# The last down-projection of an encoder trunk: the eleventh channel pair moved into the seven-product scheme, and the final norm moved into the plan

## The chip, the cores and the metric

The kernel runs on one core of a Trainium2 chip. The metric is the device time of one execution in microseconds (us), as the median of several runs. The engines named here are PE (TensorE, the matrix array), DVE (VectorE), ACT (ScalarE), POOL (GpSimd) and SP (SyncE, whose queue issues nearly all DMAs). SBUF is the on-chip memory, PSUM the small memory into which PE writes.

## The reference

A trunk of two layers over 1024 tokens of width 1024, all in float32. Each layer has a token mixer (attention in layer 0, pooling in layer 1), a cross-attention into 256 memory tokens and a gated feed-forward block; a final norm ends it. What matters here is the feed-forward block and the end:

```python
def conv_gated_ffn(h, w_up, conv_w, conv_b, w_down):
    u = h @ w_up                                   # 1024 -> 2 x 2816
    up = jnp.pad(u, ((0, 0), (1, 1), (0, 0)))
    u = up[:, :-2] * conv_w[0] + up[:, 1:-1] * conv_w[1] + up[:, 2:] * conv_w[2] + conv_b
    gate, val = u[..., :D_FF], u[..., D_FF:]
    return (jax.nn.silu(gate) * val) @ w_down      # 2816 -> 1024
...
        x = x + conv_gated_ffn(rmsnorm(x, ffn_norm[i]), ffn_w_up[i], ffn_conv_w[i],
                               ffn_conv_b[i], ffn_w_down[i])
    return rmsnorm(x, final_norm)
```

## The kernel before

**Numbers.** Each float32 operand is split into a high part (ACT, `high`) and a low part (DVE, `low`); a product of two operands is three matmuls (`mm3`: high by high, high by low, low by high). The residual stream is eight row tiles X0 to X7 of 128 tokens x 1024 columns in SBUF.

**Seven products.** The large projections are done by a scheme of Strassen's kind: a 2 x 2 product of blocks takes seven block products instead of eight, for some extra sums of operands. `PRODUCTS` names for each product its left and right operand, the PSUM bank it is added to (x, y or z), and the output that is read from that bank when it is done: "g" is the even row tile of a pair, "v" the odd one, 0 or 1 the column half. Products 2, 1 and 5 start a bank; 6, 3, 7 and 4 add to one. Each read (`read`, an add on DVE) adds the bank as it stands to the output.

**The feed-forward block** (`ffn_main`). The up-projection runs over 22 blocks f of 128 channels; behind it the convolution (ACT and DVE), the gate, and for each pair q = (2q, 2q+1) of blocks the left operands of the down-projection: four sums on DVE and seven stores of 256 KB into G7 in DRAM (`plan_gated`, `plan_sums`, `keep`). The even block of such a pair is kept in X4, the sums in X6, two row tiles that are not needed then (their rows lie in Xd in DRAM). The right operands, sums of quarters of `ffn_w_down`, were made earlier, during the cross-attention, and stored in WT (`down_sums`; `SUMS_AT` says at which weight blocks of that stage).

**Rounds.** The down-projection goes over ten pairs in three rounds (`ROUNDS`: 3, 4 and 3 pairs). In a round, for each group g of four row tiles, each of the seven products is done for two pairs of row tiles (j = 0, 1), over all pairs of the round; `plan_G` fetches and splits left operands, `plan_W` right ones, `plan_down` emits 3 matmuls of 512 columns for each pair and one read. Operands lie in 40 half tiles of SBUF: a pair's seven right operands take seven, a left operand takes two.

**The eleventh pair** (blocks 20 and 21) is done as a plain product: the gated blocks go to G (two stores of 512 KB), come back with two blocks of `ffn_w_down` (`plan_operand`), and `gemm` and `add` do 6 matmuls and one add for each row tile and column half. In layer 0 this work is handed to the next stage. In layer 1 `run` does it at the end, row tile by row tile, with the final norm one row tile behind: square on ACT (`row_rstd`), two small POOL operations, the multiply by row factor and gain on DVE (`last`, in two halves for row tile 7), and the store.

**The order of work** is not left to the engines. `Plan` takes operations with a cost per kind, gives each a due time (PE work in the order entered; others the latest time that PE's work allows, or a `late` given with them; none at all if nothing on PE follows), and emits each engine's instructions in the order in which its model would start them: the earliest possible start first, unless something with an earlier due time would be held up. Each engine, and SP's queue of DMAs, then runs its own list in order.

Of the kernel before, what the change touches and what calls it, by code (L numbers as in the profile page):

```python
# [16 lines left out]
P = 128  # L17
# [30 lines left out]
NQ = NF // 2 - 1  # L48
ROUNDS = ((0, 1, 2), (3, 4, 5, 6), (7, 8, 9))
# [579 lines left out]
class Kernel:  # L629
# [530 lines left out]
    def cross(self, i, X, steps=None, mixer=None, over={}):  # L1160
# [211 lines left out]
        def main():  # L1372
# [70 lines left out]
    def down_sums(self, i):  # L1443
# [3 lines left out]
        WT = self.WT[i] = [self.tc.dram_tile([4, P, 512], F32, name=f"Wt{i}_{q}") for q in range(NQ)]  # L1447
        raws, todo = {}, iter(range(NQ))

# [69 lines left out]
    def ffn(self, i, lhs, X, free, rhs, free_w, extra=None):  # L1519
# [6 lines left out]
        return self.ffn_main(i, U, X, Xd, extra, partial(U.begin, *self.rows_by(lhs, X, free, rhs, free_w), self.conv_table(i)))  # L1526

    def ffn_main(self, i, U, X, Xd, extra, begin):
        nc, R = self.nc, self.R
        wd = self.a["ffn_w_down"][i]  # L1530
        G = self.tc.dram_tile([2 * P, S], F32, name=f"G{i}")
        G7 = self.tc.dram_tile([NQ, P, 7 * 512], F32, name=f"Gs{i}")
# [25 lines left out]
        def held(name, f):  # L1558

            return name == "v" and f % 2 == 0 and f < 2 * NQ  # L1560
# [21 lines left out]
        def plan_gated(plan, f, late):  # L1582
            g, v = conv("g", f), conv("v", f)
            plan.add("add", 1024, partial(gated, f), g + v, v, uses=g + v, late=late)
            if f >= 2 * NQ:
                q = f - 2 * NQ
# [36 lines left out]
        def plan_G(plan, r, qs, g, n):  # L1623

            raw, parts, w = ("graw", r, g, n), [("g", r, g, n, j) for j in range(2)], len(qs) * 256
            at = PLACE.index(n) * 512 + g * 256

            def fetch():
                GA[raw] = self.scr()
                nc.sync.dma_start(out=GA[raw][:, :w].rearrange("p (q c) -> p q c", c=256),  # L1630
                                  in_=G7[qs[0]:qs[-1] + 1, :, at:at + 256].rearrange("q p c -> p q c"))

            def high():
                hs = GA[r, g, n] = [R.get_half(), R.get_half()]
                self.high(R.hv(hs[0])[:, :w], GA[raw][:, :w])

            def low():
                h, l = (R.hv(h)[:, :w] for h in GA[r, g, n])
                self.low(h, l, GA.pop(raw)[:, :w])
            plan.add("load", len(qs) / 4, fetch, [("G", q, n) for q in qs], [raw], [("scr", raw)])  # L1640
            plan.add("copy", w, high, [raw], parts, [("half", k) for k in parts], [raw])
            plan.add("add", w, low, [raw, *parts], parts, uses=[raw, *parts])
            plan.ended[parts[1]] = lambda: R.put_half(*GA.pop((r, g, n)))
# [32 lines left out]
        def plan_down(plan, r, qs, g, j, n):  # L1676
# [3 lines left out]
            b, parts, ws = (bank, r, p), [("g", r, g, left, m) for m in range(2)], [("w", q, right) for q in qs]  # L1680
            fresh = n in (2, 1, 5)

            def emit():
                if fresh:
                    banks[b] = self.psA()[:, :512] if bank == "x" else self.psB()
                hi, lo = (R.hv(x)[:, :len(qs) * 256].rearrange("p (q c) -> p q c", c=256)[:, :, j * P:(j + 1) * P]
                          for x in GA[r, g, left])
                for k, q in enumerate(qs):
                    wh, wl = U.halves(WD[q, right])
                    self.mm3(banks[b], hi[:, k], lo[:, k], wh, wl, fresh and k == 0, k == len(qs) - 1, not fresh)  # L1690

            t = 2 * p + (U.PRODUCTS[n][3] == "v")

            def read():
                x = X[t][:, h * 512:(h + 1) * 512]
                nc.vector.tensor_tensor(out=x, in0=banks[b], in1=x, op=OP.add)  # L1696
            plan.add("product", 3 * len(qs), emit, parts + ws, [b], [("A" if bank == "x" else "B", b)] if fresh else (),
                     parts + ws + ([] if fresh else [b]))
            plan.add("add", 512, read, [b, ("row", t, h)], [("row", t, h)], uses=[b], late=1.5)

        def plan_phase(plan, homes):

            home = [X[t] for t in homes]
            for t, h in enumerate(homes):
                def back(t=t):
                    X[t] = home[t]
                    nc.sync.dma_start(out=X[t], in_=Xd[t * P:(t + 1) * P, :])
                plan.add("load", 1, back, (), [(f"X{h}", j) for j in range(2)] + [("row", t, j) for j in range(2)])
            for r, qs in enumerate(ROUNDS):
                for k, q in enumerate(qs):  # L1710
                    plan_W(plan, q, -3.0 * (len(qs) - 1 - k) if k < len(qs) - 1 else None)
                for g in range(2):
                    for n in (2, 1, 5, 6, 3, 7, 4):
                        plan_G(plan, r, qs, g, U.PRODUCTS[n][0])
                    for n in (2, 1, 5, 6, 3, 7, 4):
                        for j in range(2):
                            plan_down(plan, r, qs, g, j, n)
                            yield
# [4 lines left out]
        def plan_operand(plan, kind, f, late):  # L1723
            o, parts = ("raw", kind, f), [("part", kind, f, j) for j in range(2)]

            def fetch():
                raw[kind, f] = self.scr()
                src = G[(f - 2 * NQ) * P:(f + 1 - 2 * NQ) * P, :] if kind == "g" else wd[f * P:(f + 1) * P, :]
# [12 lines left out]
        def main():  # L1741
# [8 lines left out]
            for item in U.order(NF):  # L1750
# [12 lines left out]
            for f in range(2 * NQ, NF):  # L1763
# [7 lines left out]
        ps, fs = {}, range(2 * NQ, NF)  # L1771
# [185 lines left out]
    def run(self):  # L1957
# [68 lines left out]
```

## Time and profile before

| | |
|---|---|
| Runs | 2533.35, 2533.76, 2536.28 us; median 2533.76 |
| Profiled execution | 2532.28 us, of which the span from first to last instruction 2530.5 |
| Granted TensorE clock | 0.999 |
| PE busy | 2488.5 us, 98% of the span, 13481 matmuls |
| DVE, ACT, POOL busy | 2000.4, 1347.1, 397.5 us |
| DMA | 316.25 MB, mean 125 GB/s |

The profile is of one execution. Times in it are counted from the start of the span. Groups of instructions are named by line, engine, operation and "output<-inputs" by tile name. Matmuls are pipelined: each is shown as lasting some 0.39 us, while the next begins 0.23 us after it, so a busy PE means that matmuls follow without a gap. L745, L746 and L747 are the three matmuls of `mm3`; L664 and L667 are `high` and `low`; L718 and L720 the two POOL operations of a row's norm; L726 its square; L1696 the read of a round, L1784 that of the plain product; L1994 the final multiply; L1600 the stores to G7, L1587 those to G, L1630 the loads from G7, L1654 and L1656 those of the weights, L1707 the reload of a row tile from Xd.

### The profile page before, as it was taken

How to read it: one execution, taken by the hardware profiler on the slowest of the kernel's cores; microseconds unless marked ns; L12 is line 12 of the kernel's file. 1: busy time of each engine (PE TensorE's matmuls, PEld its weight loads, DVE VectorE, ACT ScalarE, POOL GpSimd, SP SyncE). 2: the span in 40 equal slices, each digit the busy share in tenths (PEclk: the TensorE clock that was granted, in tenths of full speed). 3: DMA queues.
4: the chain of work that ended last, by engine and by line, in shares of the span. 5: the costliest groups of instructions: out<-in, count | busy, mean ns of one | idle time of the engine just before them, and what ended most of it. 6: DMA issues, size and time to landing. Idle time of an engine off the chain costs nothing.

```text
span 2530.5 us, 37018 instructions
## 1 busy us (share of the span) xinstructions
PE 2488.5 (98%) x13481; PEld 2132.1 (84%) x13481; DVE 2000.4 (79%) x2939; ACT 1347.1 (53%) x2288; POOL 397.5 (16%) x533
## 2 busy tenths in 40 slices
PE   8999999999999999999999999999999999999998
PEld 8998888888898888888887888889888888887886
DVE  7879999974886379888888776987469888887775
ACT  5558888862556255555555434655345555545441
POOL 5664545530001000000000003102000000000001
PEclk9999999999999999999999999999999999999999
DMA  4300000042595124243258663388124333338751
GB/s 158 94 18 1 1 1 1 1 159 67 169 319 196 47 87 125 84 119 111 84 163 275 204 186 110 126 282 273 66 71 117 104 100 109 104 118 264 230 187 67
DMA packets 297259, 316.25 MB, mean 125 GB/s; under 512 B 12533, under 2 KB 236125, under 8 KB 297077
## 3 DMA queue, kind: packets, MB, share of 16 engines
q1 hardware_dynamic: 297077, 313.89, 38.9%
q8 instruction: 106, 1.74, 0.3%
q14 instruction: 76, 0.62, 0.1%
HBM read 228.28 MB, written 80.74 MB: 122 GB/s over the span
## 4 chain that ended last, share of the span: by engine, by line
PE 85%; DVE 7%; issue 2%; ACT 2%; DMA 2%; POOL 1%; DVEq 0%; SPq 0%; ACTq 0%; POOLq 0%
PE pB L745 22%; PE pB L747 22%; PE pB L746 22%; PE pA L747 3%; PE pA L745 3%; PE pA L746 3%; PE pA L778 2%; DVE nm L788 2%; PE pB L739 2%; PE pB L1133 1%; DVE R L667 1%; DVE PT L673 1%; PE pB L1134 1%; ACT scr L791 1%; PE pB L323 1%
## 5 line engine op out<-in xcount | busy, mean ns | idle before, releaser
L745 PE MATMUL pB<-R,R 128*128 128x512 f32 (+1 forms) x2750 | 1023.4, 372 | 8.0 <-DVE scr L439 1.6
L746 PE MATMUL pB<-R,R 128*128 128x512 f32 (+1 forms) x2750 | 1016.1, 369 | 0.0
L747 PE MATMUL pB<-R,R 128*128 128x512 f32 (+1 forms) x2730 | 1008.9, 370 | 3.1 <-DVE R L667 3.0
L745 PEld LDWEIGHTS pB<-R,R 128*128 128x128 f32 x2750 | 518.2, 188 | 102.1 <-DVE R L667 3.4
L747 PEld LDWEIGHTS pB<-R,R 128*128 128x128 f32 x2730 | 514.3, 188 | 91.4 <-DVE R L667 4.8
L746 PEld LDWEIGHTS pB<-R,R 128*128 128x128 f32 x2750 | 518.4, 188 | 86.4 <-DVE R L673 0.3
L664 ACT ACTIVATE R<-scr 128x512 fp32r<-128x512 f32 (+2 forms) x330 | 250.2, 791 | 240.6 <-PE pB L746 56.2
L667 DVE TENSOR_TENSOR R<-X,R 128x512 fp32r<-128x512 f32 x374 | 252.7, 687 | 65.7 <-ACT R L664 65.0
L664 ACT ACTIVATE R<-X 128x512 fp32r<-128x512 f32 x374 | 231.7, 630 | 134.6 <-PE pB L746 65.2
L718 POOL TENSOR_SCALAR ms<-ss 128x1 f32<-128x1 f32 (+2 forms) x102 | 34.3, 336 | 1694.5 <-ACT R L726 661.3
L667 DVE TENSOR_TENSOR R<-scr,R 128x512 fp32r<-128x512 f32 (+2 forms) x330 | 285.1, 893 | 18.8 <-ACT R L664 18.3
L437 ACT COPY scr<-pB 128x512 f32<-128x512 f32 x156 | 91.0, 585 | 196.0 <-PE pB L747 190.9
L794 POOL TENSOR_SCALAR scr<-scr,inv 128x1024 f32<-128x1024 f32 x125 | 140.5, 1124 | 163.5 <-DVE inv L793 161.6
L673 DVE TENSOR_TENSOR PT<-pB,PT 128x512 fp32r<-128x512 f32 x256 | 163.9, 681 | 1.7 <-ACT PT L672 0.7
L1696 DVE TENSOR_TENSOR X<-pB,X 128x512 f32<-128x512 f32 x144 | 99.3, 691 | 81.2 <-PE pB L747 78.4
L791 ACT ACTIVATE scr<-pA,nm 128x1024 f32<-128x1024 f32 x125 | 139.6, 1117 | 41.3 <-DVE nm L788 40.2
L788 DVE TENSOR_REDUCE nm<-pA 128x1 f32<-128x1024 f32 x125 | 152.5, 1220 | 0.0
L745 PE MATMUL pA<-R,R 128*128 128x512 f32 (+1 forms) x416 | 149.5, 359 | 2.3 <-ACT R L664 2.3
L747 PE MATMUL pA<-R,R 128*128 128x512 f32 (+1 forms) x416 | 149.0, 358 | 0.5 <-DVE R L667 0.5
L746 PE MATMUL pA<-R,R 128*128 128x512 f32 (+1 forms) x416 | 148.6, 357 | 0.5 <-DVE R L667 0.5
L778 PE MATMUL pA<-R,R 128*128 128x512 f32 x512 | 145.1, 405 | 0.0
L672 ACT ACTIVATE PT<-pB 128x512 fp32r<-128x512 f32 x256 | 138.8, 596 | 11.1 <-PE pB L739 10.2
(152 smaller groups left out, 3510.7 us busy)
## 6 DMA issues: line engine op xcount, KB each, us to landing
X<-in_ffn_w_up SPq DMA_DIRECT2D x82, 512.0 KB
Gs<-X SPq DMA_DIRECT2D x100, 256.0 KB
scr<-in_ffn_w_down SPq DMA_DIRECT2D x44, 512.0 KB
scr<-Gs SPq DMA_DIRECT2D x56, 384.0 KB
scr<-Wt SPq DMA_DIRECT2D x40, 512.0 KB
scr<-in_xattn_w_kv SPq DMA_DIRECT2D x32, 512.0 KB
scr<-Gs SPq DMA_DIRECT2D x28, 512.0 KB
scr<-in_attn_w_qkv SPq DMA_DIRECT2D x22, 512.0 KB
```

The costliest lines, as they stand in the source:

```text
L664: self.nc.scalar.activation(hi, src, AF.Copy)
L667: self.nc.vector.tensor_tensor(out=lo, in0=src, in1=hi.bitcast(F32), op=OP.subtract)
L672: nc.scalar.activation(hi, src, AF.Copy)
L673: nc.vector.tensor_tensor(out=lo, in0=src, in1=hi.bitcast(F32), op=OP.subtract)
L745: mm(out, ah, bh, start=start, stop=False)
L746: mm(out, ah, bl, start=False, stop=False)
L747: mm(out, al, bh, start=False, stop=stop)
L778: nc.tensor.matmul(s[:, kh * 512:(kh + 1) * 512], q, R.v(K[part][kh], 4)[:, kv], start=part == 0, stop=part == 1)
L788: nc.vector.tensor_reduce(nm, s, axis=AX.X, op=OP.max, negate=True)
L791: nc.scalar.activation(pr, s, AF.Exp, bias=nm, accum_out=rs)
L794: nc.gpsimd.tensor_scalar(pr, pr, ri, 1.0, op0=OP.mult, op1=OP.mult)
L1696: nc.vector.tensor_tensor(out=x, in0=banks[b], in1=x, op=OP.add)
```

## The change

In layer 1 alone, all eleven pairs go through the rounds: 3, 4 and 4 pairs. Weight sums and activation sums are made for pair 10 too (one more place in the cross-attention of layer 1, at weight block 7), its even block lies in X4 like those of the other pairs, and the plain product of blocks 20 and 21 goes, with its stores to G and its operands. Row tiles 6 and 7, which live where X4 and X6 are, are reloaded after the first product of the first round has been entered.

The last group of the last round (row tiles 4 to 7) is done with one pair of row tiles after the other instead of both beside each other, and in the product order 1, 2, 6, 5, 7, 3, 4. Its left operands are fetched per pair of row tiles (128 tokens wide, 256 KB each, one half tile). The very last product is done in two column halves of 256.

The final norm becomes part of the plan (`plan_final`). Row tiles 0 to 6: square, multiply, store, as soon as the row tile is complete. Row tile 7: the square of its second half and the gain's multiply after product 7, the square of columns 0 to 255 (ACT) and of 256 to 511 (DVE, fused) after each half of product 4, one POOL power, then ACT scales the second half while DVE multiplies the first, and two stores.

```diff
-NQ = NF // 2 - 1
-ROUNDS = ((0, 1, 2), (3, 4, 5, 6), (7, 8, 9))
+ROUNDS = ((0, 1, 2), (3, 4, 5, 6), (7, 8, 9)), ((0, 1, 2), (3, 4, 5, 6), (7, 8, 9, 10))
+NQ = [rounds[-1][-1] + 1 for rounds in ROUNDS]
...
-                        if c in SUMS_AT:
+                        if c in (SUMS_AT if NQ[i] == 10 else (*SUMS_AT, 7)):
                             plan_sums(plan, 10.0)
...
-        def plan_G(plan, r, qs, g, n):
-            raw, parts, w = ("graw", r, g, n), [("g", r, g, n, j) for j in range(2)], len(qs) * 256
-            at = PLACE.index(n) * 512 + g * 256
+        def plan_G(plan, r, qs, g, n, js):
+            raw, parts, c = ("graw", r, g, n, js), [("g", r, g, n, js, k) for k in range(len(js))], len(js) * P
+            at, w = PLACE.index(n) * 512 + g * 256 + js[0] * P, len(qs) * len(js) * P
...
+            for m, c in enumerate(cs):
+                k, w = ((b, m) if m else b), c.stop - c.start
+                plan.add("product", 3 * len(qs) * w / 512, partial(emit, c), parts + ws, [k],
+                         [("A" if bank == "x" else "B", b)] if fresh else (), parts + ws + ([] if fresh else [b]))
+                plan.add("add", w, partial(read, c), [k, ("row", t, h)], [("row", t, h)], uses=[b], late=1.5)
+                if out is not None and r == len(rounds) - 1 and n in (3, 7, 4):
+                    plan_final(plan, t, n, m)
...
+            plan_back(range(NT - 2))
+            if out is not None:
+                plan_gain(plan)
+            for r, qs in enumerate(rounds):
                 for k, q in enumerate(qs):
                     plan_W(plan, q, -3.0 * (len(qs) - 1 - k) if k < len(qs) - 1 else None)
                 for g in range(2):
+                    end = out is not None and (r, g) == (len(rounds) - 1, 1)
+                    order = (1, 2, 6, 5, 7, 3, 4) if end else (2, 1, 5, 6, 3, 7, 4)
+                    for js in ((0,), (1,)) if end else ((0, 1),):
+                        for n in order:
+                            plan_G(plan, r, qs, g, U.PRODUCTS[n][0], js)
+                        for n in order:
+                            for j in js:
+                                plan_down(plan, r, qs, g, js, j, n, *[(slice(0, 256), slice(256, 512))] * (end and (j, n) == (1, 4)))
+                                yield
+                                if (r, g, n, j) == (0, 0, 2, 0):
+                                    plan_back(range(NT - 2, NT))
...
+            def rest():
+                s, x = last[t], X[t][:, 256:512]
+                nc.vector.scalar_tensor_tensor(junk(("fjunk", t, 2))[:, 256:512], x, 1.0 / D, x, op0=OP.mult, op1=OP.mult,
+                                               accum_out=s[:, 2:3])
+                nc.vector.tensor_tensor(out=s[:, 2:3], in0=s[:, 2:3], in1=s[:, 0:1], op=OP.add)
+            def root():
+                s = last[t]
+                nc.gpsimd.tensor_tensor(out=s[:, 3:4], in0=s[:, 2:3], in1=self.mh[:, :1], op=OP.pow)
...
+            if t < NT - 1 and n in (3, 4):
+                j = ("fjunk", t)
+                plan.add("square", 1024, square, row, [r], [("half", j)], [j])
+                plan.add("tap", 1024, lambda: scaled(t, last[t], slice(0, 1024)), [r, "gain", *row], row, uses=["gain"])
+                plan.add("load", 1, lambda: leave(t, slice(0, 1024)), row)
+            elif t == NT - 1 and n == 7:
+                plan_part("square", 512, partial(part, 0, hi), 0, row[1:], [(r, 0)])
+                plan.add("add", 512, gained, ["gain", *row[1:]], row[1:], uses=["gain"])
+            elif t == NT - 1 and not m:
+                plan_part("square", 256, partial(part, 1, slice(0, 256)), 1, row[:1], [(r, 1)])
+                plan.add("tiny", 1, sums, [(r, 1)], [(r, 0)])
+            elif t == NT - 1:
+                plan_part("tap", 256, rest, 2, [(r, 0), *row[:1]], [(r, 2)])
+                plan.add("scale", 1, root, [(r, 2)], [r])
+                plan.add("copy", 512, other, [r, *row[1:]], row[1:])
+                plan.add("tap", 512, lambda: scaled(t, last[t][:, 3:4], lo), [r, "gain", *row[:1]], row[:1], uses=["gain"])
+                for c, k in ((hi, row[1:]), (lo, row[:1])):
+                    plan.add("load", 0.5, partial(leave, t, c), k)
...
-                    plan_gated(plan, f, {0: 4.0, 1: 8.0, 2: 12.0, NF - 2: 8.0, NF - 1: 4.0}.get(f, 14.0))
+                    plan_gated(plan, f, {0: 4.0, 1: 8.0, 2: 12.0, 2 * nq: 8.0, 2 * nq + 1: 4.0}.get(f, 14.0))
...
-        gemm, add, _ = self.ffn(1, lhs, X, *ops)
-        gain = self.bcast(a["final_norm"])
-        def rest(t):
-            for n in range(2):
-                gemm(t, n)
-                add(t, n)
-        def last(t):
-            h = self.scr()
-            r = self.row_rstd(X[t], h)
...
-        skewed(NT, (0, rest), (1, last))
+        self.ffn(1, lhs, X, *ops, out=self.out[0])
```

More of the change, by code (lines that the diff above doesn't have):

```diff
@@ L1517, in conv_table, with ffn @@
         return turn
-    def ffn(self, i, lhs, X, free, rhs, free_w, extra=None):
+    def ffn(self, i, lhs, X, free, rhs, free_w, extra=None, out=None):
         nc, R, a = self.nc, self.R, self.a
@@ L1692, in plan_down @@
[L1692 to L1699, printed above, removed]
+                    wh, wl = (w[:, c] for w in U.halves(WD[q, right]))
@@ new lines, in emit, with read @@
+                    self.mm3(banks[b][:, c], hi[:, k], lo[:, k], wh, wl, fresh and k == 0, k == len(qs) - 1, not fresh)
+            def read(c):
+                x = X[t][:, h * 512 + c.start:h * 512 + c.stop]
+                nc.vector.tensor_tensor(out=x, in0=banks[b][:, c], in1=x, op=OP.add)
+            for m, c in enumerate(cs):
[5 more added lines that the diff above has]
+                    plan_final(plan, t, n, m)
@@ L1762, in main @@
                     extra(plan)
-            for f in range(2 * NQ, NF):
+            for f in range(2 * nq, NF):
                 for kind in "dg":
```

112 lines of the change are left out of this document (68 added, 44 removed).

## The prediction

> **What bounds the kernel now.** I read the summary of the profile first, then the chain that ended last, then stretches of the last layer, then single instructions at its end. Summary, chain and costliest rows:
>
> ```profile
> PE 2488.5 (98%) x13481; PEld 2132.1 (84%) x13481; DVE 2000.4 (79%) x2939; ACT 1347.1 (53%) x2288; POOL 397.5 (16%) x533
> ...
> PE 85%; DVE 7%; issue 2%; ACT 2%; DMA 2%; POOL 1%; DVEq 0%; SPq 0%; ACTq 0%; POOLq 0%
> ```
>
> TensorE (PE) is busy for 98% of the span and carries 85% of the chain. Only three things can therefore move the time by more than noise: how many matmul cycles are issued, where PE waits, and what stands after the last matmul. The next view gives busy time per engine in stretches of the last layer; the last three numbers are the granted clock, the DMA share and GB/s (the first row is for PE alone).
>
> ```profile
> 1688.00:1712.00 24.00, 24.00 (x203) 1.00 0.95 326
> 1744.00:1768.00 24.00, 23.77 (x179) 22.15 (x178) 14.44 (x29) 13.89 (x41) 3.68 (x8) 1.00 0.72 246
> 2294.00:2316.00 22.00, 18.89 (x77) 14.13 (x78) 17.70 (x24) 12.60 (x18) 0.00 (x0) 1.00 0.87 301
> 2316.00:2336.00 20.00, 20.00 (x90) 16.54 (x89) 16.32 (x23) 10.85 (x16) 0.00 (x0) 1.00 0.90 286
> 2365.00:2384.00 19.00, 19.00 (x86) 15.73 (x85) 16.34 (x21) 9.75 (x11) 0.00 (x0) 1.00 0.93 308
> 2403.00:2422.00 19.00, 19.00 (x86) 15.72 (x85) 14.37 (x22) 10.28 (x17) 0.00 (x0) 1.00 0.49 157
> 2441.00:2519.00 78.00, 77.93 (x344) 64.19 (x343) 44.89 (x58) 16.19 (x23) 5.23 (x11) 1.00 0.23 77
> 2520.00:2530.50 10.50, 0.21 (x1) 0.00 (x0) 5.74 (x7) 2.30 (x4) 2.29 (x4) 0.68 0.50 200
> ```
>
> Two places are not filled with matmuls: the hand-over from the up-projection to the down-projection (2294 to 2316: 22.00 - 18.89 = 3.11 us of PE idle) and the 10.5 us at the end. From 2441 to 2519, the third round and the plain matmuls behind it, PE runs without a gap, at 78.00 / 344 = 0.2267 us per matmul of 512 columns. In that stretch VectorE (DVE) is busy 45 of 78 us and DMA hardly works. The end, by instruction (start, duration, engine, line, operation):
>
> ```profile
> 2519.82 0.39 PE L747 MATMUL pB<-R,R 128*128 128x512 f32 x1
> ...
> 2521.16 1.88 DVE L1784 TENSOR_TENSOR X<-pB,X 128x512 f32<-128x512 f32 x3
> 2524.02 1.28 DVE L1994 SCALAR_TENSOR_TENSOR scr<-X,rs,scr 128x1024 f32<-128x1024 f32 x1 [0.98 <-POOL rs L720]
> 2526.02 1.42 DVE L1994 SCALAR_TENSOR_TENSOR scr<-X,rs,scr 128x512 f32<-128x512 f32 x2 [0.72 <-POOL rs L720]
> ...
> 2523.12 1.06 ACT L726 ACTIVATE scr<-X 128x1024 f32<-128x1024 f32 x1
> 2524.08 0.19 ACT L726 ACTIVATION_READ_ACCUMULATOR scr<-X 128x1 f32 x1
> ...
> 2523.16 0.19 POOL L718 TENSOR_SCALAR ms<-ss 128x1 f32<-128x1 f32 x1 [3.24 <-ACT scr L726]
> ...
> 2524.35 1.00 POOL L718 TENSOR_SCALAR ms<-ss 128x1 f32<-128x1 f32 x1 [0.37 <-ACT scr L726]
> 2525.43 0.55 POOL L720 TENSOR_TENSOR rs<-ms,mh 128x1 f32<-128x1 f32 x1
> ```
>
> The last matmul ends at 2519.82 + 0.39 = 2520.21, so the tail is 2530.5 - 2520.21 = 10.29 us. Its parts: DVE is behind and ends the last add at 2523.04 (2.83 us after PE); square and accumulator read until 2524.27; GpSimd (POOL) until 2525.98; two half multiplies until 2527.44; then 3.06 us in which the last store is issued and lands.
>
> **The change part by part.** Prices come from this execution (span 2530.5, own time 2532.28, so 1.78 us lie around the span). The median of the runs shown, 2533.76, is 1.48 us above it.
>
> *Matmuls.* The plain product of pair 10 goes: 8 row tiles x 2 halves x 2 blocks x 3 = 96 matmuls. The third round grows from 3 pairs to 4: 7 products x 4 pairs of row tiles x 3 = 84 more. 12 x 0.2267 = 2.72 us less on PE, which nothing hides. **-2.72.**
>
> *Last product in two column halves.* 12 matmuls of 512 columns become 24 of 256. The stretch 1688 to 1712 is all 256 columns: 24.00 / 203 = 0.118 us each; 24 x 0.118 = 2.84 against 12 x 0.2267 = 2.72. **+0.12.** Both halves are in one PSUM tile, and DVE reads the first while PE should write the second. No such pair exists before. Lower end 0 (columns kept apart); upper end a read of 0.42 behind a 1.28 us multiply of another tile, 1.7. A matmul has waited for a read of its own tile, in the fourth row here:
>
> ```profile
> PE pA L745 <- ACT R L664: 1.4, 2, 1.2
> PE pB L747 <- DVE R L667: 1.0, 1, 1.0
> PE pB L745 <- DVE X L1696: 0.3, 1, 0.3
> PE pB L745 <- ACT scr L437: 0.3, 1, 0.3
> ...
> L667 DVE TENSOR_TENSOR R<-pB,R 128x256 fp32r<-128x256 f32 x48 | 19.6, 420 | 13.8 <-ACT R L664 13.5
> L1816 DVE SCALAR_TENSOR_TENSOR scr<-scr,pgain 128x256 f32<-128x256 f32 x8 | 3.6, 478 | 0.0
> L793 DVE RECIPROCAL inv<-sum 128x1 f32<-128x1 f32 x125 | 19.7, 157 | 14.2 <-ACT scr L791 13.9
> L1457 DVE TENSOR_TENSOR scr<-scr 128x512 f32<-128x512 f32 x40 | 27.7, 693 | 1.7 <-DMA scr<-in_ffn_w_down 1.0
> ```
>
> (It is the L1696 row; the last four rows are groups with their mean ns.) I take one bare read, 0.42, plus some 0.1 of hand-over at each side as between ACT's end at 2524.27 and POOL's start at 2524.35: **+0.55.** In the Trainium skill, "PSUM — Partial Sum Buffer", section "PSUM bank collisions raise a hardware error", two engines may not touch one bank at a time even at different columns, so that software has to order them. By that rule the wait is there, 0.55 or more; without it the sum would be 0.55 better. No row before the change decides it.
>
> *The tail.* For row tile 7 the square of its second half and the multiply by the gain are done while product 4 runs, so after the last matmul stand: the add of 256 columns (0.42), the sums and the fused square of 256 columns (0.48, L1816 row; two one-column operations at 0.16 each, L793 row), POOL's power (0.08 to start, 0.55), the multiply of 512 columns (half of 1.42 and a start, 0.75; ACT's copy-with-scale of the other half lies beside it) and the store (3.06). One thing stands in between: row tile 6 is complete only after product 3, 2.72 us ahead of the end. Its add, square and POOL step (0.69, 1.25, 0.8) use that up, so its multiply of 1024 columns (1.28) is ready just when the add of the last columns is. Both have no due time, the planner takes what can start first, and by its costs (square 2.36 us after 0.72 for the add) that is tile 6, half a microsecond ahead of tile 7's sums. Sum: 0.45 + 1.28 + 0.16 + 0.48 + 0.16 + 0.63 + 0.75 + 3.06 = 6.97 against 10.29: **-3.3.** Without tile 6 in front it is 5.7, a gain of 4.6; if POOL is held for 1.0 us as at 2524.35 the gain is 2.3.
>
> *Last group by single row tiles.* With one row tile at a time, the products on one bank are only one other product apart: DVE has 12 x 0.2267 = 2.72 us for the read before PE needs the bank again, where it had twice that. Per product DVE must do a read (0.69), the low half of one operand (0.69) and, for a while, one multiply of the final norm (1.28): 2.66 of 2.72. The reads carry due times and the multiplies none, so they mostly fit; but a multiply queued on DVE waits for POOL, and then the reads wait behind it. Lower end 0; upper end 0.8 (1.00 - 0.19, the two L718 rows) for three of the eight places, 2.4. I take **+0.5.** ACT has 0.63 + 1.25 of 2.72, and the operands come in 256 KB pieces where the stretch 2441 to 2519 moved 77 GB/s: both cost nothing as long as PE itself is full.
>
> *Hand-over, 2294 to 2316.* DMA issues of SP and the PE waits there:
>
> ```profile
> 2278.55 0.93 SPq L1707 DMA_DIRECT2D X<-Xd  x2
> ...
> 2295.28 0.36 SPq L1630 DMA_DIRECT2D scr<-Gs  x1
> 2295.69 1.01 SPq L1587 DMA_DIRECT2D G<-scr  x1
> ...
> 2314.47 0.32 SPq L1587 DMA_DIRECT2D G<-scr  x1
> ...
> 2303.56 0.50 PE L745 MATMUL pA<-R,R 128*128 128x512 f32 x1 [1.16 <-ACT R L664]
> ...
> 2315.36 0.50 PE L747 MATMUL pB<-R,R 128*128 128x512 f32 x1 [1.00 <-DVE R L667]
> ```
>
> Removed: the two stores of 512 KB and the early due times of the last two gate products (one of 1.22 us stood on DVE at 2313, just ahead of the 1.00 us wait). Moved: channel block 20's values lie in X4, not in a scratch tile, so a scratch tile is free from about 2279 to 2298, while the first operand load of the round was issued only at 2295; the reload of row tiles 6 and 7 (1 MB at 2278) goes behind the first product. Added: four sums on DVE (4 x 0.69 = 2.8) and seven stores of 256 KB on SP's queue, due some 15 us later, where DVE is busy 16.32 of 20 us: 3.7 idle, which covers the sums barely. What they hold up is the reload of tiles 6 and 7, needed only 14 products (about 28 us) into the round. Ends: all 3.11 us of idle vanish, or the 2.8 us of sums land on PE. I take a third of the idle: **-1.0.**
>
> *Weight sums of pair 10 in the cross-attention.* Two loads of 512 KB, four subtractions (2.8 us of DVE) and four stores of 256 KB at about 1745 to 1768, where PE idles 0.23 us, DVE is busy 14 of 24 and DMA 0.72. 2 MB at 326 GB/s are 6.4 us of DMA. SP's queue has the output weights and the returning rows behind it, which are used from about 1792 on. Ends: 0 and all 6.4; with 0.23 us of PE idle in 24 us the row is near the lower end. **+0.2.** The splits of pair 10 (7 + 7 of 512 columns for 4 of 1024) and 16 fewer adds lie beside PE in a stretch with DVE at 45 of 78: 0. The gain vector is fetched earlier and holds one of six scratch tiles: 0. Layer 0 keeps its rounds; only the order of entering two loads moves: 0.
>
> Sum: -2.72 + 0.12 + 0.55 - 3.3 + 0.5 - 1.0 + 0.2 = **-5.65 us.** From 2532.28 that is 2526.6; on the scale of the median 2528.1, 0.22% faster. About 0.2% (5.07 us) is what a measurement of this kernel can tell from no change, so the forecast is just past it.
>
> **The rivals.**
>
> *DVE behind POOL in the last group* (no change). Seven row tiles' norms now run between products. For it: the two L718 rows, 0.19 us with DVE idle and 1.00 us while the multiply of 2524.02 ran. If each of the seven puts 0.8 us on PE, 5.6 us go back: -0.05, 2533.7. Against it: before the change the same norms ran behind plain products and PE did not wait once from 2441 on. The Trainium skill, "SBUF — State Buffer", section "Who interferes with whom", says that a VectorE instruction with two SBUF inputs and a GpSimd instruction that reads SBUF shut each other out for the whole instruction; the two L718 rows agree with it. By that rule the 0.8 us recur at each collision. Chance 0.18.
>
> *The hand-over or the tail gives nothing* (no change). The sums and later loads put 2.8 us on PE instead of -1.0: -1.85, 2531.9. For it: DVE at 17.70 and 16.32 of 22 and 20 us. Or the tail gains 2.3 and the idle stays: -3.65, 2530.1. Chance 0.16.
>
> *Operands of the four-pair round come too slowly* (slower). The last round now needs 4 x 1792 KB of weights and 14 x 512 KB of gated values, 14.7 MB, in 336 x 0.2267 = 76.2 us: 193 GB/s. If SBUF halves come free so late that the supply is that of 2403 to 2422, 157 GB/s, it takes 93.6 us: +17.4 - 5.65, 2545.5. It decides from 10.7 us of loss on, a supply under 169 GB/s. Against it: the second round already has four pairs, moved 308 GB/s when it had to, and PE was full. Chance 0.09. That fewer matmuls are issued can't fail; the count is fixed by the code.
>
> **How the numbers follow.** Forecast 0.57, rivals 0.18, 0.16 and 0.09. Faster by over 0.2%: the forecast, 0.57. Within 0.2%: the two rivals between, 0.34. Slower: 0.09. The range takes the lower ends of hand-over (another -2.1) and tail (another -1.3), and a little for the median: 2523; upwards it includes the first two rivals and 2 us of the runs' own spread: 2536. Only the slower rival lies outside.
>
> **What would show it.** Right: about 7 us from the last matmul to the end; one PE wait near 0.5 us between the 256-column matmuls; PE otherwise full over the last 76 us; less than 3 us idle around 2294 to 2316; tile 6's multiply on DVE ahead of tile 7's fused square. Wrong: PE waits on DVE's reads at several places of the last group, new waits in the first round or in the cross-attention of layer 1, or a tail that is still 9 us or more.

## The result and the profile after

The changed kernel takes 2542.01 us (median of 11 runs, 2539.76 to 2543.97) against 2535.03 us for the kernel before (11 runs, 2532.81 to 2537.70). The ratio is 1.0027, with a 95% interval of 1.0018 to 1.0036: about 7 us slower, where 5.65 us faster was forecast. The profiled execution took 2542.65 us, its span 2540.9.

The summary of the profile after, stretches of it (as before: duration, then busy time and count by engine, granted clock, DMA share, GB/s), and what ACT waited for near the end:

```profile
PE 2486.5 (98%) x13481; PEld 2132.1 (84%) x13481; DVE 1998.7 (79%) x2946; ACT 1350.8 (53%) x2301; POOL 402.6 (16%) x532
...
PE 82%; DVE 9%; ACT 3%; DMA 3%; issue 3%; POOL 1%; SPq 0%; DVEq 0%; POOLq 0%; ACTq 0%
...
2441.00:2519.00 78.00, 78.00 (x357) 65.06 (x355) 35.47 (x52) 13.68 (x21) 0.00 (x0) 1.00 0.25 76
2520.00:2541.00 21.00, 0.00 (x0) 0.00 (x0) 10.89 (x13) 8.88 (x19) 13.49 (x15) 0.60 0.50 200
...
ACT R L1768 <- DVE X L1699: 32.9, 1, 32.9
```

PE is as full as before in the last round: 78.00 of 78.00 us. But POOL does nothing there (0.00), where it did 5.23 us of norms before; now 13.49 us of POOL's work stand behind the last matmul. And ACT waited 32.9 us in one piece. The end of the changed kernel, by instruction (L1699 is the read, L1768 a part of row tile 7's square, L726 the square of a whole row tile, L1747 the final multiply):

```profile
2518.93 0.28 PE L747 MATMUL pB<-R,R 128*128 128x256 f32 x1
...
2516.37 0.69 DVE L1699 TENSOR_TENSOR X<-pB,X 128x512 f32<-128x512 f32 x1 [2.03 <-PE pB L747]
2519.24 0.75 DVE L1699 TENSOR_TENSOR X<-pB,X 128x256 f32<-128x256 f32 x2 [2.18 <-PE pB L747]
2522.26 1.28 DVE L1747 SCALAR_TENSOR_TENSOR X<-X,rs,scr 128x1024 f32<-128x1024 f32 x1 [2.26 <-POOL rs L720]
2524.26 1.28 DVE L1747 SCALAR_TENSOR_TENSOR X<-X,rs,scr 128x1024 f32<-128x1024 f32 x1 [0.72 <-POOL rs L720]
...
2536.47 0.75 DVE L1747 SCALAR_TENSOR_TENSOR X<-X,ss,scr 128x512 f32<-128x512 f32 x1 [0.44 <-POOL ss L1786]
...
2519.76 0.42 ACT L1768 ACTIVATE R<-X 128x256 fp32r<-128x256 f32 x1 [32.90 <-DVE X L1699]
2520.18 1.04 ACT L726 ACTIVATE R<-X 128x1024 fp32r<-128x1024 f32 x1
...
2521.39 0.19 POOL L718 TENSOR_SCALAR ms<-ss 128x1 f32<-128x1 f32 x1 [635.45 <-ACT R L726]
2522.43 1.16 POOL L718 TENSOR_SCALAR ms<-ss 128x1 f32<-128x1 f32 x1 [0.21 <-ACT R L726]
2523.67 0.55 POOL L720 TENSOR_TENSOR rs<-ms,mh 128x1 f32<-128x1 f32 x1
2524.31 1.29 POOL L718 TENSOR_SCALAR ms<-ss 128x1 f32<-128x1 f32 x1
```

The last matmul ends at 2518.93 + 0.28 = 2519.21, and the tail is 2540.9 - 2519.21 = 21.7 us against 10.29 before. The first norm instruction on ACT is row tile 7's square of columns 0 to 255, which needs the very last product; the other eight squares stand behind it in ACT's list, though six of the row tiles had been complete for 19 us or more (the last read of row tiles 4 and 5 starts at 2500.05). Then six whole row tiles follow each other at 2.0 us (multiplies from 2522.26 to 2532.27): two POOL operations and the multiply of each, and from the second tile on POOL's first operation takes 1.16 to 1.29 us instead of 0.19, beside DVE's multiply of the tile before. Row tiles 6 and 7 end the list, with multiplies at 2534.74 and 2536.47.

The hand-over from the up-projection and the first rounds, PE's waits from 2270 to 2375 and the busy time of that stretch, changed kernel:

```profile
PE pB L745 <- DVE X L1699: 2.6, 1, 2.6
PE pB L747 <- DVE R L667: 1.3, 1, 1.3
...
2270.00:2375.00 105.00, 100.97 (x442) 1.00 0.80 263
```

The five waits between 2294 and 2305 are gone. One of 1.3 us has come at 2325.7 (1.0 before, at 2315), and one of 2.6 us at 2362, at the start of the second round. One part of the 10.4 us between the two profiled spans belongs to the execution and not to the change. The first row of each pair here is a stretch in the cross-attention of layer 1 (PE alone), before and then after; the second the transposes of the convolution table (behind the three durations: first and last start).

```profile
1580.00:1600.00 20.00, 18.63 (x156) 1.00 0.27 108
L1514 PE MATMUL pB<-ident,scr x8: 232/233/255, 853.1 to 1822.2; 44*128 44x44 f32 x8
...
1580.00:1600.00 20.00, 19.78 (x156) 0.91 0.25 99
L1514 PE MATMUL pB<-ident,scr x8: 232/232/255, 853.4 to 1824.6; 44*128 44x44 f32 x8
```

The profiled execution after had a granted clock of 0.91 in one stretch and was 2.4 us late at 1824.6, ahead of everything that the change touches on PE. The same matmul was 1.0 us late ahead of that stretch (1584.56 before, 1585.56 after) and 2.3 us late behind it (1616.51, 1618.80), so the stretch itself cost 1.3 us. The run e7 below has the changed kernel's code up to there; its granted clock was 1.00 in that stretch and its last transpose starts at 1822.1, as before the change. From 1824.6 on PE needed 694.6 us to its last matmul, before 698.0: 3.4 us less. So the span's account is +2.4 (this execution), -3.4 (PE), +11.4 (tail) = +10.4.

### The profile page after: what moved, and what is told of

Same layout as the page of the kernel before. It is cut to its first block, busy times and chain, and to the rows that moved or that the text cites. A ratio compares the mean times of both kernels' runs of the same rounds, so it can differ in the third digit from the quotient of the medians.

```text
span 2540.9 us, 37074 instructions
## 1 busy us (share of the span) xinstructions
PE 2486.5 (98%) x13481; PEld 2132.1 (84%) x13481; DVE 1998.7 (79%) x2946; ACT 1350.8 (53%) x2301; POOL 402.6 (16%) x532
## 4 chain that ended last, share of the span: by engine, by line
PE 82%; DVE 9%; ACT 3%; DMA 3%; issue 3%; POOL 1%; SPq 0%; DVEq 0%; POOLq 0%; ACTq 0%
PE pB L745 21%; PE pB L747 21%; PE pB L746 21%; PE pA L747 3%; PE pA L745 3%; PE pA L746 3%; PE pA L778 2%; DVE nm L788 2%; PE pB L739 2%; DVE R L667 2%; PE pB L1133 1%; DVE PT L673 1%; PE pB L1134 1%; ACT scr L791 1%; ACT R L664 1%
## 5 line engine op out<-in xcount | busy, mean ns | idle before, releaser
L1699 DVE TENSOR_TENSOR X<-pB,X 128x512 f32<-128x512 f32 (+1 forms) x145 | 99.2, 686 | 87.2 <-PE pB L747 85.6
```

Of the source, the lines that this page charges most:

```text
L1699: nc.vector.tensor_tensor(out=x, in0=banks[b][:, c], in1=x, op=OP.add)
```

## The experiments

The ratios are against the kernel before, measured beside each. "Tail" is the time from the end of the last matmul to the end of the span in the profiled execution.

**e1: due times for the norm.** The planner starts nothing on an engine other than PE earlier than 30 us ahead of its due time (L260: `max(t, op["due"] - self.AHEAD)`). For an operation without a due time that is infinity less 30. Such an operation is emitted after everything that has one, and so stands behind all of it in its engine's list.

```diff
         def plan_final(plan, t, n, m):
+            add = partial(plan.add, late=6.0)
...
-                plan.add("square", 1024, square, row, [r], [("half", j)], [j])
+                add("square", 1024, square, row, [r], [("half", j)], [j])
```

(and so for each operation of `plan_final`).

> Only edit to the changed kernel: every operation of the final norm gets a due time of 6 us behind its product. Theory A (operations without a due time are put behind everything that has one): the norms of row tiles 0 to 5 run before the last matmul, the time from the last matmul to the end falls from 21.7 us to about 7, PE still ends some 3 us earlier than before on the same scale; ratio to before about 0.997. Rival B (POOL and DVE lock each other out, about 2.0 us for each row tile, wherever the norms stand): the collisions move under the last group and hold up reads, at least 5 us of new PE waits appear there; ratio 0.999 or more.

Measured: 2527.61 us, ratio 0.9973 (0.9964 to 0.9982). The last instructions, in the same views as above:

```profile
2517.86 0.28 PE L747 MATMUL pB<-R,R 128*128 128x256 f32 x1
...
2518.18 0.76 DVE L1699 TENSOR_TENSOR X<-pB,X 128x256 f32<-128x256 f32 x2 [1.58 <-PE pB L747]
2518.85 1.27 DVE L1747 SCALAR_TENSOR_TENSOR X<-X,rs,scr 128x1024 f32<-128x1024 f32 x1
2520.04 0.21 DVE L1777 TENSOR_SCALAR ss<-ss 128x1 f32<-128x1 f32 x1
...
2517.35 0.19 POOL L718 TENSOR_SCALAR ms<-ss 128x1 f32<-128x1 f32 x1 [15.52 <-ACT R L726]
2520.86 0.55 POOL L1787 TENSOR_TENSOR ss<-ss,mh 128x1 f32<-128x1 f32 x1 [2.69 <-DVE ss L1783]
```

The tail is 2525.7 - 2518.14 = 7.6 us, and PE has no wait in the last group at all. Theory A holds and rival B falls: POOL takes 0.19 us again, because DVE isn't multiplying at that moment. That one argument turned a loss of 0.27% into a gain of 0.27%.

**e6: which instruction blocks.** The square of tile 7's first columns did have a due time in the changed kernel, though none was given. It reads the row's first half, and the read of the last 256 columns, which has a due time, writes that half in the planner's book; so the square has to come before it. Here it is entered behind that read:

```diff
                 plan.add("add", w, partial(read, c), [k, ("row", t, h)], [("row", t, h)], uses=[b], late=1.5)
+            for m, _ in enumerate(cs):
                 if out is not None and r == len(rounds) - 1 and n in (3, 7, 4):
                     plan_final(plan, t, n, m)
```

> The changed kernel, still without due times, with one edit: row tile 7's square of columns 0 to 255 is entered in the plan behind the last read instead of ahead of it, so that the read no longer follows it and it gets no due time through the read. Theory C (the one instruction with a due time stands first on ACT, waits there for the first half of the last product, and all squares stand behind it): the squares and POOL steps of row tiles 0 to 5 move under the last group; the multiplies on DVE still stand behind the last read, so the tail falls from 21.7 us to 12 to 18, ratio to before 0.999 to 1.001. Rival (the missing due times alone put everything behind the end): the tail stays at 20 us or more.

Measured: 2534.12 us, ratio 1.0005 (0.9996 to 1.0014). ACT, POOL and DVE:

```profile
2492.34 1.06 ACT L726 ACTIVATE R<-X 128x1024 fp32r<-128x1024 f32 x1 [1.66 <-PE pB L747]
...
2493.58 0.19 POOL L718 TENSOR_SCALAR ms<-ss 128x1 f32<-128x1 f32 x1 [1.98 <-ACT R L726]
...
2517.51 7.26 DVE L1748 SCALAR_TENSOR_TENSOR X<-X,rs,scr 128x1024 f32<-128x1024 f32 x6
```

The squares now run under the last group, the multiplies still in a row behind the last read (7.26 us for six). The last matmul ends at 2516.80, so the tail is 2532.7 - 2516.8 = 15.9. So 21.7 - 15.9 = 5.8 us of the tail were the one square at the head of ACT's queue, and 15.9 - 7.6 = 8.3 us the multiplies and stores held behind the last read for want of due times.

**e5: no plan for the norm at all.** `plan_final` isn't called; the norm is written behind the plan, row tile by row tile, as before the change, and the last group is done like the others.

```diff
-        self.ffn(1, lhs, X, *ops, out=self.out[0])
+        self.ffn(1, lhs, X, *ops)
+        gain = self.bcast(a["final_norm"])
+        def last(t):
+            h = self.scr()
+            r = self.row_rstd(X[t], h)
...
+        skewed(NT, (0, last))
```

> All eleven pairs in rounds, the last group like the others, and the final norm not planned: written row tile by row tile behind the plan, as in the kernel before. Theory A: the changed kernel's norms run as if unplanned, so this takes the same tail, 20 to 23 us from the last matmul, ratio to before 1.002 to 1.004. If planning the norm did bring something: a tail 3 us or more longer than the 21.7 of the changed kernel.

Measured: 2527.61 us, ratio 0.9975 (0.9966 to 0.9984), a tail of 8.7 us. My expectation was wrong. The code orders by hand only inside the plan (`manual_schedule`); the norm stands behind it, and the trace shows its multiplies between the reads:

```profile
2508.61 1.29 DVE L2084 SCALAR_TENSOR_TENSOR scr<-X,rs,scr 128x1024 f32<-128x1024 f32 x1 [2.21 <-POOL rs L720]
2509.81 0.68 DVE L1699 TENSOR_TENSOR X<-pB,X 128x512 f32<-128x512 f32 x1
```

So nearly all of the gain comes with the eleventh pair. The norm planned with due times, together with the new order of the last group (e1), is 1.1 us better in the tail and not distinguishable in the time; planned without them, it was worse than not planned.

**e2: row tile 7 ahead of row tile 6.** As e1, `late=6.0 if t < NT - 1 else 0.0`.

> As e1_due, but row tile 7's operations are due at once (0 us), so that they are emitted ahead of row tile 6's multiply on DVE. Theory A with the tail as it was worked out in the prediction: 0.5 to 1.3 us less tail than e1_due. If the order of tiles 6 and 7 doesn't matter because the last store sets the end either way: the same tail within 0.3 us.

Measured: 2528.20 us, ratio 0.9981 (0.9972 to 0.9989); tail 2530.3 - 2521.27 = 9.0 us, 1.5 more and not 0.5 to 1.3 less. Rows of POOL, DVE and SP:

```profile
2522.98 1.28 DVE L1747 SCALAR_TENSOR_TENSOR X<-X,rs,scr 128x1024 f32<-128x1024 f32 x1
2524.70 0.75 DVE L1747 SCALAR_TENSOR_TENSOR X<-X,ss,scr 128x512 f32<-128x512 f32 x1 [0.44 <-POOL ss L1787]
...
2523.14 1.53 POOL L1787 TENSOR_TENSOR ss<-ss,mh 128x1 f32<-128x1 f32 x1 [1.85 <-DVE ss L1783]
...
2525.45 1.30 SPq L1750 DMA_DIRECT2D out<-X  x3
```

Tile 6's multiply, now behind tile 7's sums, held off POOL's power for tile 7 (1.53 us against 0.55), and tile 6's store of 512 KB was issued with tile 7's two at the very end. The last multiply ends at 2525.45 and the span 4.85 us later, where 3.06 had been enough before the change.

**e3: the last product in one piece.** As e2, with 12 matmuls of 512 columns and one read at the end (row tile 7's operations behind the two halves are entered together); row tile 6's multiply comes out ahead of tile 7's sums again.

```diff
-                                plan_down(plan, r, qs, g, js, j, n, *[(slice(0, 256), slice(256, 512))] * (end and (j, n) == (1, 4)))
+                                plan_down(plan, r, qs, g, js, j, n)
```

> As e2_due_t7first, with the very last product done as 12 matmuls of 512 columns and one read. If the two halves lie in one bank and the read of the first waits for the matmuls of the second (in the changed kernel both reads stand together behind the last matmul), the halving buys nothing: within 0.5 us of e2_due_t7first in the tail, and PE 0.1 us less. If the halves do overlap: 0.5 to 1.0 us more tail than e2_due_t7first.

Measured: 2525.73 us, ratio 0.9970 (0.9958 to 0.9981), a tail of 7.6 us. That is 1.4 us less than e2 and lies outside both branches of the expectation, because the edit also put row tile 6 first again: the order of the tail is that of e1, so e1 is the one to compare with, with 7.6 us there too. The halving buys nothing, as both reads of the halves stood behind the last matmul ("x2" at 2518.18 in e1, at 2519.24 in the changed kernel). This is the shortest of the versions that compute everything, though its interval overlaps those of e1 and e5.

**e7: what holds POOL off.** The changed kernel, tiles 0 to 6 multiplied by ACT and without the gain.

```diff
-                plan.add("tap", 1024, lambda: scaled(t, last[t], slice(0, 1024)), [r, "gain", *row], row, uses=["gain"])
+                plan.add("copy", 1024, lambda: nc.scalar.activation(X[t], X[t], AF.Copy, scale=last[t]), [r, "gain", *row], row, uses=["gain"])
```

> The changed kernel with the multiply of row tiles 0 to 6 done by ACT with the row factor alone; the multiply by the gain is left out for these tiles. DVE then has nothing large to do behind the last read. If POOL's first norm operation took 1.29 us because DVE's multiply held it off: 0.19 us now for each tile, as where DVE is idle. If it is slow for another reason (waiting on its own results): still above 1 us. The time says nothing here; square and scale follow each other on ACT, some 3.3 us for each tile.

Measured (2546.39 us in a single run): the first POOL operation takes 0.19 us for every one of the seven tiles; one of them:

```profile
2524.61 0.19 POOL L718 TENSOR_SCALAR ms<-ss 128x1 f32<-128x1 f32 x1 [2.31 <-ACT R L726]
```

So it is DVE's multiply, with two inputs in SBUF, that held POOL off: in the changed kernel POOL's operation of 2524.31 ends at 2525.60 and the multiply beside it (2524.26) at 2525.54. This is the rule of the Trainium skill, "SBUF — State Buffer", section "Who interferes with whom", and the trace agrees with it: 0.19 us against 1.29.

**e8, e9, e10, e11, e13: the waits near 2325 and 2362.** All start from e3, where PE waits 1.0 us near 2325 and 2.0 us near 2362. e8 puts the old due times of blocks 20 and 21 back:

```diff
-                    plan_gated(plan, f, {0: 4.0, 1: 8.0, 2: 12.0, 2 * nq: 8.0, 2 * nq + 1: 4.0}.get(f, 14.0))
+                    plan_gated(plan, f, {0: 4.0, 1: 8.0, 2: 12.0, NF - 2: 8.0, NF - 1: 4.0}.get(f, 14.0))
```

> As e3_no_halves, with the due times of the gate products of blocks 20 and 21 in layer 1 put back to 8 and 4 us, as before the change. Theory D (their convolution, sums, seven stores and the two reloads, postponed by some 10 us, fall into the stretch 2312 to 2335 in which DMA and DVE are full, and the operands of the second round come late): the PE wait of 2.0 us near 2362 falls under 0.5, the wait of 1.0 us near 2325 moves or goes, and up to 2 us of waits come back between 2290 and 2316: the total of PE waits from 2290 on is between 1 and 2.5 us against 3.0. Rival (the second round's own supply): the wait at 2362 stays at 1.5 or more.

e9 leaves out pair 10's four sums and seven stores (the line for the even block's store has the same condition):

```diff
-                plan_sums(plan, f // 2, v, late + 3.0)
+                if f // 2 < 10:
+                    plan_sums(plan, f // 2, v, late + 3.0)
```

> As e3_no_halves, with the four sums and seven stores of pair 10's left operands left out; the last round then reads pairs 6 to 9 in place of 7 to 10, so the output is not the reference's. Theory D: without that work both waits, 1.0 us near 2325 and 2.0 us near 2362, fall under 0.5 us together. If only the second round's supply sets the wait at 2362, it stays at 1.5 or more and only the one at 2325 goes.

e10 leaves out the stores alone (`q < 10 and plan.add("load", ...)` in `plan_sums`, and the same for the store of the even block), e11 the sums alone (`add` does nothing for q = 10):

> As e3_no_halves, pair 10's four sums kept and its seven stores left out; the last round reads pairs 6 to 9 in place of 7 to 10, so the output is not the reference's. If DVE's 2.8 us for the sums make the waits near 2325 and 2362: they stay, 1.0 and 1.5 to 3 us. If the 1.75 MB of stores in a full DMA stretch make them: both under 0.5 us, as without either.

> As e3_no_halves, pair 10's four sums left out and its seven stores kept, which then store old sums, so the output is not the reference's. If DVE's sums make the waits: both under 0.5 us. If the stores do: they stay, 1.0 and 1.5 to 3 us.

e13 has neither, as e9, but keeps their tiles occupied:

```diff
+                else:
+                    def touch():
+                        nc.vector.tensor_tensor(out=fixed[1][:, :1], in0=C["v", f - 1][:, :1], in1=C["v", f][:, :1], op=OP.add)
+                    plan.add("tiny", 1, touch, [*v, ("X4", 0), ("X4", 1)], [("X6", 0), ("X6", 1)], uses=[v[0]], late=late + 5.0)
```

> As e9_no_sums10 (pair 10's sums and stores left out, the last round reads pairs 6 to 9, the output is not the reference's), with one addition of a single column on DVE that reads blocks 20 and 21 and writes X6, due when the last of the stores would be: the scratch tile of block 21, X4 and X6 stay held, and the reloads of row tiles 6 and 7 stay behind them. If the holding makes the waits near 2325 and 2362: they come back, 1.0 and 1.5 us or more, PE waits 2.5 us or more from 2270 to 2375. If the work itself does, of DVE or of the stores: 0.5 us or less, as in e9_no_sums10.

Measured, all for the stretch 2270 to 2375 (PE alone), in the order e3, e8, e9, e10, e11, e13:

```profile
2270.00:2375.00 105.00, 101.86 (x446) 1.00 0.81 269
...
2270.00:2375.00 105.00, 101.29 (x444) 1.00 0.79 263
...
2270.00:2375.00 105.00, 105.00 (x464) 1.00 0.81 270
...
2270.00:2375.00 105.00, 102.38 (x448) 1.00 0.74 246
...
2270.00:2375.00 105.00, 101.07 (x434) 0.98 0.81 263
...
2270.00:2375.00 105.00, 104.80 (x463) 1.00 0.77 255
```

(The granted clock was 0.98 in e11's row.) PE idles 3.1 us in e3, 3.7 with the early due times (ratio 0.9978, 0.9969 to 0.9987), nothing without sums and stores (0.9961, 0.9946 to 0.9977), 2.6 with sums alone (0.9972, 0.9962 to 0.9983), 3.9 with stores alone (0.9977, 0.9968 to 0.9986) and 0.2 with the tiles held and no work (0.9954, 0.9937 to 0.9971). Kernels with the same hand-over differ by as much among themselves, from 2.6 us (e1, e6) to 4.0 (the changed kernel), so only the step from these down to 0 and 0.2 says something; the intervals of the times overlap.

With the early due times the wait near 2325 goes, 2.2 us come at 2312 and 2318 in its place, and the one near 2362 stays at 1.5 us: theory D in that form falls. Nor does the holding of X4, X6 and a scratch tile make the waits, as far as e13 tests it: the two reloads were issued at 2328.01 and 2329.92 (2330.80 and 2331.71 in the changed kernel, where PE was 2.7 us further on with its work), and PE hardly waited. With the sums alone both waits are there, 1.0 and 1.5 us, as in e1. With the stores alone the one near 2362 is there, 1.6 us, the one near 2325 is 0.5, and 1.9 us of others stand between 2301 and 2304. I had expected one of the two to be innocent.

What PE waits for is DVE. Rows of DVE in the changed kernel (L1608 is one of pair 10's sums):

```profile
2324.61 0.68 DVE L1608 TENSOR_TENSOR X<-X 128x512 f32<-128x512 f32 x1
2325.32 0.69 DVE L1608 TENSOR_TENSOR X<-scr,X 128x512 f32<-128x512 f32 x1
2325.93 1.55 DVE L667 TENSOR_TENSOR R<-scr,R 128x768 fp32r<-128x768 f32 x2
...
2360.61 3.10 DVE L667 TENSOR_TENSOR R<-scr,R 128x512 fp32r<-128x512 f32 x5 [0.95 <-ACT R L664]
2363.62 0.68 DVE L1699 TENSOR_TENSOR X<-pB,X 128x512 f32<-128x512 f32 x1
```

The split at 2325.93, for which PE waits, stands behind the sums; the read at 2363.62, for which PE waits 2.6 us, stands behind five splits in a row in DVE's list (seven, 4.3 us, in e1, e10 and e11; three, 1.9 and 2.4 us, in e13 and e9). Why the planner's order comes out so with the sums or the stores alone, and what a full DMA adds, is not settled.

**e12: row tile 6's multiply in two parts.** From e3, gain on DVE right after the square, row factor on ACT:

```diff
+                if t == NT - 2:
+                    def gain6():
+                        nc.vector.tensor_tensor(out=X[t], in0=X[t], in1=last["gain"], op=OP.mult)
+                    add("add", 1024, gain6, ["gain", *row], row, uses=["gain"])
+                    add("copy", 1024, lambda: nc.scalar.activation(X[t], X[t], AF.Copy, scale=last[t]), [r, *row], row)
```

> As e3_no_halves, row tile 6's multiply taken apart: by the gain on DVE as soon as its square is done, by the row factor on ACT. In the tail DVE's multiply of tile 6 (1.28 us) stood between the last read and tile 7's sums; it begins 1 us earlier now, so the tail falls from 7.6 to about 6.6 us, if POOL's power for tile 6 is not held off by it; if it is, ACT's 1.15 us for tile 6 end later than tile 7's own chain and the tail stays within 0.3 us of 7.6.

Measured: 2528.17 us, ratio 0.9975 (0.9965 to 0.9985), tail 8.0 us. The multiply by the gain stayed behind the last read (it starts at 2519.64, the read at 2519.03), so nothing was gained: the tail is 0.4 us longer than e3's and outside both branches of the expectation. The reason I had given for that, POOL being held off, was not it; POOL's operations for tile 6 took 0.19 and 0.55 us.

## Why the prediction was wrong

**The step that failed is "The tail".** It said that the multiplies "have no due time, the planner takes what can start first", and it worked out only which of row tiles 6 and 7 would then come first on DVE. The code says otherwise in one line: the start of an operation is not before its due time less 30 us, and without a due time that is never, until nothing with a due time is left. The prediction noted that the norm's operations have no due time and that the planner starts what it can, and did not put the first together with the limit of 30 us. All eight row tiles, and not two of them, were left behind the last matmul; +11.4 us stood in the place of -3.3. Of the 11.4, 5.8 us came from the one square at the head of ACT's list, which had a due time by way of the last read (e6). That was in no term of the sum. Nor did the order come out as worked out: in the changed kernel tile 6's multiply (2534.74) stood behind tile 7's fused square (2534.20). e1 gives the operations due times and nothing else; there tile 6 comes first and the tail is 7.6 us against the 6.97 worked out. The pair of reads took 0.35 us more than in the sum, the stores at the end 0.45 more, the rest 0.2 less.

**Matmuls, -2.72 and +0.12: right.** The trace has 24 matmuls fewer of 512 columns and 24 more of 256, at 0.2267 and 0.12 us; from the convolution table to the last matmul PE needed 3.4 us less, of which 2.6 are these and 0.4 the hand-over's (below).

**The two column halves, +0.55: a wrong place.** PE didn't wait between them. The row on which the term rested (L1696, the third of its fence and not the fourth) shows such a wait of 0.3 us for a read, but here the first half's read waited for the second half's matmuls: 2.18 us of idle DVE in front of the pair of reads at 2519.24. By the planner's costs the second half can start on PE 0.2 us ahead of the first half's read, so it is emitted first; that this order decides who waits was not tested. By the Trainium skill, "PSUM — Partial Sum Buffer", section "PSUM bank collisions raise a hardware error", software has to keep two engines out of one bank, and the trace agrees that they were kept apart. The wait costs nothing on PE and makes the halving worthless (e3 against e1).

**Last group, +0.5: nothing.** No PE wait in the last 76 us in the changed kernel, nor with the norms under that group in e1. The first rival, DVE behind POOL, falls with it: DVE's multiply does hold POOL off (e7), but with due times the planner spread the norms so that no read held PE up. (That PE ran without a gap from 2441 to 2519 before the change is not quite what the row shows: 77.93 of 78.00 us.)

**Hand-over, -1.0: of that size, but not by that sum.** Counted by the same matmuls, PE was 2.3 us late ahead of the hand-over (2290.12 before, 2292.43 after), 2.2 us early at 2318.00 (2315.76) and 1.9 us late again at the end of the second round (2440.10, 2442.05). The waits of the last blocks did vanish, as worked out, and were worth 4.6 us; pair 10's sums and stores made two others that took 4.2 us back, the upper end of that step and more. So the changed kernel gained 0.4 us here; the same hand-over gained 1.2 us in e7, 1.3 in e3, 1.8 in e1 and 2.1 in e6. That the difference of two such terms came near -1.0 is partly luck. PE's idle time from 2270 to 2375 went the other way by the profile, from 3.51 to 4.03 us, in part because it leaves out the slow start behind each wait: 0.34 us lie between the first two matmuls after one (2364.36 and 2364.70) and 0.23 between later ones, and there were seven waits before and two after.

**Cross-attention, +0.2: nothing.** From 1740 to 1800 PE idles 0.8 us before and after.

**The rivals.** The slower one, a supply too slow for the four-pair round, had no part in the result: PE was full from 2365 on. The side of the result came from a mechanism that was not among the rivals. With due times the ratio comes out near the forecast, 0.9973 in e1 against 0.9978, in part because errors cancel: the tail gained 2.7 us and not 3.3, and the 1.25 us priced for the halves, the last group and the cross-attention didn't appear.

## What to carry to other kernels

In an order written out ahead of time, look for every operation that nothing urgent follows, the output side above all: find out what the planner does with one that has no deadline, and give it one. Read each engine's list as a queue: one instruction that waits for the last result, at the head of the queue, holds back everything behind it however long that has been ready, and in the profile it shows as one long idle time with a late releaser (32.9 us on ACT here), not as a busy engine. When a change has two parts, price and run each by itself: the eleventh pair alone was worth 0.25% (e5), which the other part hid.

## What the runs showed of the hardware that was not expected

POOL's power of one column took 0.55 us with DVE idle, 1.53 us beside one multiply of 1024 columns on DVE (e2), and 1.45, 1.47 and 2.07 us beside a row of six of them (e6). That is 2.6 to 3.8 times as long.

```profile
2518.93 1.45 POOL L720 TENSOR_TENSOR rs<-ms,mh 128x1 f32<-128x1 f32 x1 [19.81 <-DVE X L1748]
...
2523.70 2.07 POOL L720 TENSOR_TENSOR rs<-ms,mh 128x1 f32<-128x1 f32 x1
```

The granted clock of 0.91 over the stretch 1580 to 1600 shows in seven of the fourteen profiled executions (the changed kernel, e1, e2, e6, e10, e12, e13) and not in the other seven; rows of the same height show elsewhere, such as at 2360 to 2380 in e2 and e5. In the changed kernel it is one short piece, with a mean clock of 0.53 from 1592.0 to 1595.6. It delayed PE there by 1.3 us, and in e6 by 1.5 us, a fifth of the whole effect. What sets it off is open; it stands ahead of the change. Two profiled spans are not enough to tell 0.3%; the position of the same instruction in both, ahead of the change, tells what to take off.
